# A decoder layer on one core: filling steps dealt by weight between attention steps, and one head group's last value product moved behind the branch products

## The chip, the cores and the metric

The kernel runs on one core of a Trainium2 chip. A core has a matrix engine (TensorE: PE in the profile, its weight loads as PEld), a vector engine (VectorE: DVE), an activation engine (ScalarE: ACT), a general engine (GpSimd: POOL) and a queue engine (SyncE: SP) that here only starts transfers. TensorE writes to PSUM, eight accumulators ("banks") of 128 x 512 float32 values; DVE and ACT read PSUM and write to the on-chip buffer SBUF. The metric is the device time of one execution in microseconds (us); lower is better.

## The reference, cut to what matters

One layer is computed for 512 tokens with 16 "meta" tokens ahead of them, model width 1024: a gated feed-forward (FFN) of inner width 2816, a token mixer, and a second FFN, each added to the residual. The change is inside the token mixer:

```python
qa, ka, va, fa, qb, kb, vb, ga, gb = jnp.split(h @ w_in, idx, axis=-1)   # q and k then RMS-normalised per head
# forgetting attention: 8 heads of 64, causal over the whole sequence
s = q @ k.T * scale + c[q] - c[k];      o_fox = softmax(mask(s)) @ v
# sliding attention: 8 query heads, 2 key/value heads, a band of 128 keys and the 16 meta tokens
s = q @ k.T * scale + bias;             o_swa = softmax_with_sink(mask(s)) @ v
y = sigmoid(ga) * (o_fox @ w_branch_fox) + sigmoid(gb) * (o_swa @ w_branch_swa)
return y @ w_out
```

All values are float32; a product is made as three TensorE passes on a high and a low part of each operand.

## The kernel before, in words

**Products.** Each operand x is kept as a high part (a rounded copy, made by ACT: `hi`, line 133 or 134) and a low part (x minus the high part, made by DVE: `lo`, lines 140 and 142). `prod` (lines 301, 302, 304) issues high x high, high x low and low x high into one PSUM bank. A weight piece lands by DMA in `raw`, is split by `hi` and `lo` into `wh` and `wl`, and is then used; `piece()` hands out the next piece and starts the loads and splits of later ones.

**Attention units.** The forgetting attention has eight units (four pairs of heads, and for each pair two pairs of query blocks), made by `fox_pair`. A unit is five steps: `scores` (products of queries with keys, line 1292; DVE adds the forgetting sums and finds the row minimum, line 1310; ACT takes exponentials, line 1209; DVE divides by the sums, line 1212), and then, for each of the two heads, `turn` (TensorE transposes the probabilities, lines 1337 and 1350; ACT and DVE split the result into `pH` and `pL`) and `values` (products with the values, lines 1359, 1364 and 1365; `both_halves`, lines 1105 and 1106, brings the two partition halves together into `oA`). The *first* `turn` of a unit is that of head 0, the *second* that of head 1. A unit of the later query blocks has seven transposes in its second `turn`, one of the earlier blocks three. The sliding attention has eight units of three steps (`swa_unit`): `scores` (DVE: line 1460), one `turn` for all four heads of a group (line 1473) and one `values` (lines 1488 and 1490).

**Stages and filling.** The units are dealt into four lists, `main[0]` to `main[3]`: four forgetting units, four more, four sliding units of group 0, four of group 1. The next unit's `scores` stands between the first `turn` of a unit and its first `values`. While an attention step waits for DVE and ACT, TensorE is to have other work: the lists in `fills`. Fills 0 to 2 are steps that project keys, queries, values and gates of later units (half a token block, or a quarter of a gate: 12 products of 256 columns or 6 of 512); fill 3 holds the 16 steps of the forgetting branch products (`foxes`: six products of 512 columns each, eight output blocks of two steps). `weave(main, fill)` writes the two lists into one: after main step i of n, the fills up to share i/n of their number.

**What sets the order.** The written order is a priority. The framework's planner lays each engine's instructions out ahead of the run on a modelled clock, so an instruction whose inputs it takes to be late can be passed by a later one of the same engine; it also assigns the buffers in the order in which they are given back. `after(i)` puts instructions behind i on their engine. On the chip each engine then keeps to its planned order.

**Behind the attention.** After the weaving come, in written order: sigmoids of three gate blocks `zA` on ACT (line 1653; the activation tables change here from exponential to sigmoid) and their products with the forgetting branch (DVE, line 1654); `stM.close()`, after which the stage's SBUF is used again by the pool `gates`, each tile as soon as the old tiles at its place are no longer used; differences of the mixer's input in `spare` (DVE, lines 1695 and 1696); the reload of the residual `xg` (two transfers on ACT's queue, line 1700); the last gate block's product, half before and half behind `split_o`, which splits the sliding result `oA` into `oW` and `oLs`; six sliding branch products, with copies back to `oA` (line 1722); scaling of `xg` (ACT, line 1728), sums of it (DVE, line 1732), their splits into S3, S2 and S1; and then the gate products (`seven`) that use S3 and the split sums `tc` of weights (lines 233 and 234).

**Places.** `spare` takes the place of transposed-probability inputs `t` and of the sliding values `v`; `xg` that of the two query buffers `qH`, one of which holds the low part of the forgetting result to the last of the branch products; the weight buffers `rawC` that of `pL`.

Of the kernel before, what the change touches and what calls it, by code (L numbers as in the profile page):

```python
# [55 lines left out]

def weave(main, fill):

    done, out = 0, []
    for i, f in enumerate(main):  # L60
        out.append(f)
        upto = (i + 1) * len(fill) // len(main)
        out += fill[done:upto]
        done = upto
    return out


def nothing():
# [8 lines left out]
def run(steps):  # L77
    for f in steps:
        f()
# [3 lines left out]
def kernel(  # L83
# [32 lines left out]
    def nm(s):  # L116
        nid[0] += 1
        return f"{s}_{nid[0]}"
# [489 lines left out]
    def after(*ins):  # L608

        st = ExitStack()  # L610
        for i in ins:
            st.enter_context(tc.issue_after(getattr(i, "ins", i)))
        return st
# [166 lines left out]
    def early(X, ff, dsts, second, sums, more, alone=0):  # L780


        u = [ff.plain(d, i == 0 and not alone) for i, d in enumerate(dsts)]
        main = u[0][:4] + u[1][:2]
        if alone:
            main[1:1] = [enter_rest]
        run(main[:alone] + second[:3] + main[alone:] + second[3:] if alone else weave(main, second))
        run(weave(u[0][4:] + [s for v in ([u[1][2:]] + u[2:]) for s in v], sums + more))
# [460 lines left out]
    def fox_pair(box, p, ip, before):  # L1249
# [115 lines left out]
                PE.matmul(pv[:, a:256], st, pL[:, c0 + a : c0 + 256], start=False, stop=j == nt - 1)  # L1365
            both_halves(oA[half[hh], 0, p, 2 * P * ip : 2 * P * (ip + 1)], half[hh], pv[:, :256])

        return [scores] + [lambda f=f, hh=hh: f(hh) for hh in range(2) for f in (turn, values)]

# [162 lines left out]
    for i in every:  # L1534
# [3 lines left out]
            out=zf[:n, i], in0=ps[:, 256:264], scalar=r1[:n, i : i + 1], in1=fb[:n], op0=ALU.mult, op1=ALU.add  # L1538
# [64 lines left out]
    def fox_out(m):  # L1603

        return zA[:, m] if m >= NG - 1 else oF["f"][m // 2][:, S * (m % 2) : S * (m % 2) + S]

    class Later:
# [10 lines left out]
    ]  # L1618
    parts = [
        [fox_pair(f0, p, ip, pre(p, ip)) for p in range(2) for ip in (1, 0)],  # L1620
        [fox_pair(f1, p, ip, pre(p, ip)) for p in range(2, 4) for ip in (1, 0)],
        [swa_unit(sw, q2, 0, i, swa_pre.get(i, nothing)) for i in range(NB)],
        [swa_unit(sw, q3, 1, i, nothing) for i in range(NB)],
# [11 lines left out]
    main = [[] for _ in parts]  # L1635
# [10 lines left out]
    run(main[0][:1] + fills[0][:2])  # L1646
    del main[0][:1], fills[0][:2]
    main[3].insert(0, fox_parts)
    for m, f in zip(main, fills):
        run(weave(m, f))  # L1650
    for m in range(NG - 1):
        with after(shared["exp"]):
            A.activation(zA[:, m], zA[:, m], AF.Sigmoid)
        V.tensor_tensor(out=zA[:, m], in0=zA[:, m], in1=fox_out(m), op=ALU.mult)
# [13 lines left out]
    part = lambda name: gp.tile([P, 2, 4, HF], F32R, tag=name, name=nm(name))  # L1668
# [352 lines left out]
```

## Time and profile before

| | |
|---|---|
| median of 3 runs | 1077.91 us (1076.78 to 1078.76) |
| profiled execution | 1075.97 us |
| its span, first to last instruction | 1074.2 us |
| TensorE matmul / weight loads, share of the span | 99% / 96% |
| DVE, ACT, POOL | 83%, 61%, 20% |
| granted TensorE clock | 0.999 |

The profiled execution lasts 1.77 us longer than its span. TensorE matmuls overlap: the start-to-start distance of two products of 256 columns is some 0.12 us while each is shown with 0.28 us, so a busy matmul row hides short waits, and a wait is read from the distance of starts. "[0.33 <-DVE pL L140]" behind an instruction says that its engine sat idle for 0.33 us until the DVE instruction of line 140 on `pL` was done. The attention with its filling runs from about 405 to 595 us, the last gate block and the sliding branch products from 595 to 618 us.

### The profile page before, as it was taken

Reading aid. Unit: us, or ns where it says so; the run is one execution under the profiler, and the core shown is the slowest. Engines: PE = TensorE matmul, PEld = TensorE weight load, DVE = VectorE, ACT = ScalarE, POOL = GpSimd, SP = SyncE. Lnnn points to the kernel's source line nnn. Section 1 sums busy time; section 2 is a strip of 40 time slices with the busy share of each in tenths; the row PEclk is TensorE's granted clock in tenths of the full one; section 3 lists DMA queues with packets and bytes.
Section 4 is the critical chain, followed back from the end, with each engine's and each line's share of the span. In section 5 each row is a group of like instructions: output and inputs, shape, how many; then the busy total and the mean of one; then the engine's idle time right before and its main releaser. Section 6 shows DMA issues by size and latency. Waiting matters only on the chain.

```text
span 1074.2 us, 22262 instructions
## 1 busy us (share of the span) xinstructions
PE 1062.6 (99%) x8515; PEld 1030.1 (96%) x8515; DVE 891.9 (83%) x1725; ACT 654.5 (61%) x1235; POOL 212.6 (20%) x281
## 2 busy tenths in 40 slices
PE   9999999999999999999999999999999999999998
PEld 8999999999999999999877799999999999999998
DVE  7988878888889678789897799778989788887895
ACT  7667456656666455556657776555665466745664
POOL 3011111121124442332200110001122211221120
PEclk9999999999999999999999999999999999999999
DMA  8787778688776314212211874556689777887763
GB/s 281 203 220 160 189 192 197 152 221 216 176 178 178 122 60 132 72 56 81 81 59 50 233 186 121 193 195 197 166 202 187 185 190 182 179 191 191 160 126 101
DMA packets 112570, 173.57 MB, mean 162 GB/s; under 512 B 10880, under 2 KB 59264, under 8 KB 112208
## 3 DMA queue, kind: packets, MB, share of 16 engines
q1 hardware_dynamic: 74464, 122.72, 36.0%
q0 software_dynamic: 29040, 37.83, 22.5%
q10 hardware_dynamic: 8960, 11.60, 3.4%
q8 instruction: 66, 1.08, 0.4%
q14 instruction: 40, 0.33, 0.1%
HBM read 167.89 MB, written 6.32 MB: 162 GB/s over the span
## 4 chain that ended last, share of the span: by engine, by line
PE 45%; DVE 4%; DMA 3%; ACT 3%; issue 1%; POOL 0%; ACTq 0%; DVEq 0%; POOLq 0%
PE ps L301 8%; PE ps L304 8%; PE ps L302 8%; PE pt L301 6%; PE pt L302 6%; PE pt L304 6%; DMA raw<-in_wout_dram 1%; DVE wl L140 1%; ACT wh L133 1%; DMA xg<-h1d 1%; ACT t L1209 1%; DVE pL L140 1%; ACT xg L1728 0%; PE ps L1473 0%; PE ps L1936 0%
## 5 line engine op out<-in xcount | busy, mean ns | idle before, releaser
L301 PE MATMUL ps<-x,wh 128*128 128x256 f32 (+2 forms) x768 | 219.9, 287 | 0.2
L302 PE MATMUL ps<-x,wh 128*128 128x256 f32 (+2 forms) x768 | 219.1, 285 | 0.5 <-DVE x L142 0.4
L304 PE MATMUL ps<-x,wl 128*128 128x256 f32 (+2 forms) x768 | 219.1, 286 | 0.0
L140 DVE TENSOR_TENSOR wl<-raw,wh 128x1024 fp32r<-128x1024 f32 (+3 forms) x125 | 150.0, 1201 | 39.7 <-ACT wh L133 38.4
L133 ACT CAST wh<-raw 128x1024 fp32r<-128x1024 f32 (+3 forms) x125 | 128.4, 1029 | 87.6 <-PE ps L302 50.9
L301 PEld LDWEIGHTS ps<-x,wh 128*128 128x128 f32 x768 | 144.9, 189 | 1.6 <-ACT hT L686 0.3
L302 PEld LDWEIGHTS ps<-x,wh 128*128 128x128 f32 x768 | 144.7, 188 | 1.4 <-DVE x L142 0.9
L304 PEld LDWEIGHTS ps<-x,wl 128*128 128x128 f32 x768 | 144.7, 188 | 0.8
L301 PE MATMUL pt<-x,wh 128*128 128x256 f32 (+2 forms) x424 | 125.4, 297 | 0.5 <-ACT wh L133 0.5
L304 PE MATMUL pt<-x,wl 128*128 128x256 f32 (+2 forms) x424 | 124.6, 295 | 0.0
L302 PE MATMUL pt<-x,wh 128*128 128x256 f32 (+2 forms) x392 | 112.7, 288 | 0.0
L133 ACT CAST wh<-tc 128x1024 fp32r<-128x1024 f32 (+1 forms) x70 | 71.8, 1026 | 65.4 <-DVE tc L234 56.1
L140 DVE TENSOR_TENSOR wl<-tc,wh 128x1024 fp32r<-128x1024 f32 (+1 forms) x70 | 83.5, 1193 | 32.4 <-ACT wh L133 32.2
L301 PE MATMUL ps<-acts,wh 128*128 128x264 f32 (+1 forms) x352 | 100.5, 286 | 0.1
L304 PE MATMUL ps<-acts,wl 128*128 128x264 f32 (+1 forms) x352 | 99.9, 284 | 0.0
L302 PE MATMUL ps<-acts,wh 128*128 128x264 f32 (+1 forms) x352 | 99.6, 283 | 0.0
L140 DVE TENSOR_TENSOR wl<-rawC,wh 128x1024 fp32r<-128x1024 f32 (+1 forms) x70 | 84.2, 1203 | 5.8 <-ACT wh L133 5.5
L133 ACT CAST wh<-rawC 128x1024 fp32r<-128x1024 f32 (+1 forms) x70 | 71.6, 1023 | 22.6 <-PE pt L302 16.7
L301 PEld LDWEIGHTS pt<-x,wh 128*128 128x128 f32 x424 | 80.0, 189 | 2.8 <-ACT wh L133 0.7
L304 PEld LDWEIGHTS pt<-x,wl 128*128 128x128 f32 x424 | 79.8, 188 | 2.1
L302 PEld LDWEIGHTS pt<-x,wh 128*128 128x128 f32 x392 | 73.8, 188 | 0.6
L301 PEld LDWEIGHTS ps<-acts,wh 128*128 128x128 f32 x352 | 66.6, 189 | 0.7 <-DVE h2T L918 0.3
(442 smaller groups left out, 3241.3 us busy)
## 6 DMA issues: line engine op xcount, KB each, us to landing
rawC<-in_w1i_dram SPq DMA_DIRECT2D x20, 512.0 KB, 4.3
raw<-in_w1i_dram SPq DMA_DIRECT2D x40, 256.0 KB, 4.6
raw<-in_w2i_dram SPq DMA_DIRECT2D x40, 256.0 KB, 3.5
rawC<-in_w2i_dram SPq DMA_DIRECT2D x20, 512.0 KB, 4.3
raw<-in_wm_dram SPq DMA_DIRECT2D x18, 512.0 KB, 4.2
raw<-in_wout_dram SPq DMA_DIRECT2D x16, 512.0 KB, 4.4
rawD<-in_w1i_dram SPq DMA_DIRECT2D x20, 256.0 KB, 3.9
raw<-in_w1i_dram POOLq DMA_DIRECT2D x20, 256.0 KB, 4.6
```

Source lines behind the costliest of these rows:

```text
L133: return A.copy(o, i)
L140: return V.tensor_tensor(out=o, in0=i, in1=h, op=ALU.subtract)
L301: PE.matmul(ps, sH, mH, start=first, stop=False, **more)
L302: PE.matmul(ps, sH, mL, start=False, stop=False, **more)
L304: shared["mm"] = PE.matmul(ps, sL, mH, start=False, stop=last, **more)
L1209: shared["exp"] = A.activation(t, t, AF.Exp, bias=nmx, scale=-1.0, accum_out=l[:, j : j + 1])
```

## The change: what it does

```diff
 def weave(main, fill):
 
-    done, out = 0, []
-    for i, f in enumerate(main):
+    done, out, part = 0, [], 0.0
+    share = [getattr(f, "share", 1.0) for f in main]
+    for f, s in zip(main, share):
         out.append(f)
-        upto = (i + 1) * len(fill) // len(main)
+        part += s
+        upto = len(fill) if f is main[-1] else int(part * len(fill) / sum(share) + 0.5)
         out += fill[done:upto]
         done = upto
     return out
+
+
+def shared_out(f, share):
+
+    def step():
+        f()
+
+    step.share = share
+    return step
...
-        return [scores] + [lambda f=f, hh=hh: f(hh) for hh in range(2) for f in (turn, values)]
+        shares = ((turn, 0, 1.0), (values, 0, 0.5), (turn, 1, 2.0), (values, 1, 0.5))
+        return [scores] + [shared_out(lambda f=f, hh=hh: f(hh), s) for f, hh, s in shares]
...
     main[3].insert(0, fox_parts)
+    last_values = main[3].pop()
     for m, f in zip(main, fills):
         run(weave(m, f))
+    last_values()
     for m in range(NG - 1):
```

A step now has a weight. A forgetting unit's second `turn` has 2, its two `values` 0.5 each, every other step 1, so a unit's sum stays 5; the fills are dealt by the weights gone by, rounded to the nearest instead of downward. Of the unit whose steps stand in the middle of `main[1]`, the written order goes from the first line to the second (F is a filling step, T and V the head's turn and values, S the next unit's scores):

```
before: T0 F S F V0 F T1 F V1 F
after:  T0 F S F V0 F T1 F F V1
```

Elsewhere the rounding moves single fills by one place; in `main[2]` the sliding steps keep the weight 1, and the first sliding turn has five fills behind its scores instead of four. The number of filling steps in each list, and every instruction, stay as they are.

Second, the last sliding unit's `values` leaves `main[3]` and is called after all steps of `foxes`. The end of that list goes, in written order, from the first line to the second (S15, T15 and V15 are the last sliding unit's steps, V14 the values of the one before, and 5b to 7b the branch products' steps):

```
before: S15 5b V14 6a T15 6b V15 7a 7b
after:  S15 6a 6b V14 7a T15 7b V15
```

## The prediction

> **What bounds the kernel now.** I read the page's head first, then the stages of the attention, then who TensorE waited for there.
>
> ```profile
> span 1074.2 us, 22262 instructions
> PE 1062.6 (99%) x8515; PEld 1030.1 (96%) x8515; DVE 891.9 (83%) x1725; ACT 654.5 (61%) x1235; POOL 212.6 (20%) x281
> ```
>
> TensorE is the bound over the whole run; only its waits can be won. The busy times of the two attention stretches:
>
> ```profile
> 405.00:530.00 125.00, 122.79 (x1022) 115.85 (x1021) 103.28 (x315) 73.81 (x188) 35.69 (x73) 1.00 0.28 85
> 530.00:595.40 65.40, 64.43 (x367) 50.63 (x366) 54.99 (x156) 45.15 (x113) 0.95 (x1) 1.00 0.18 58
> ```
>
> The columns are PE, PEld, DVE and ACT. Matmuls fill 122.79 of 125 us and 64.43 of 65.4 us, and DVE is busy for 83% and 84%: a second engine close behind. Next, PE's waits between 405 and 625 us, and then those of its weight loads:
>
> ```profile
> PE pt L1365 <- DVE pL L140: 1.0, 3, 0.5
> PE ps L1292 <- DVE qn L1073: 0.5, 1, 0.5
> PE pt L1488 <- ACT pH L133: 0.5, 1, 0.5
> PE pt L301 <- ACT wh L133: 0.5, 1, 0.5
> PE ps L301 <- ACT pt L529: 0.4, 1, 0.4
> PE ps L1473 <- DVE t L1212: 0.3, 1, 0.3
> ```
>
> ```profile
> PEld pt L1365 <- DVE pL L140: 2.1, 5, 0.7
> ```
>
> The longest wait is the one that the change is aimed at: value products (L1365) that wait for the low part `pL`. One of them, with its chain:
>
> ```profile
> 474.05 0.49 PE L1350 MATMUL ps<-ident,t 128*128 128x128 f32 x3
> ...
> 475.79 0.28 PE L1359 MATMUL pt<-pH,v 128*128 128x256 f32 x1
> ...
> 476.02 0.28 PE L301 MATMUL ps<-wh,x 128*128 128x256 f32 x1
> ...
> 477.10 0.38 PE L1365 MATMUL pt<-pL,v 128*128 128x256 f32 x1 [0.33 <-DVE pL L140]
> ...
> 474.88 0.48 ACT L133 CAST pH<-ps 128x384 fp32r<-128x384 f32 x1
> ...
> 475.65 0.60 DVE L1073 SCALAR_TENSOR_TENSOR qn<-hsq,r,hss 16x128 f32<-16x128 f32 x2
> 476.18 0.40 DVE L1106 TENSOR_TENSOR oA<-ps,hsq 64x256 f32<-64x256 f32 x1
> 476.51 0.54 DVE L140 TENSOR_TENSOR pL<-ps,pH 128x384 fp32r<-128x384 f32 x1
> ```
>
> The second transposition starts at 474.05, its values at 475.79, and the first product with `pL` at 477.10: 3.05 us after the transposition. `pH` was ready at 475.36, but DVE had a filling step's scaling (L1073) and an earlier head's sum (L1106) in its queue and came to `pL` 1.15 us later. At 476.02 the plan has let filling products (L301) pass the products with `pL`; it still took `pL` to be earlier than it was.
>
> **Part 1, the weights.** Behind a second transposition stand now one fill, afterwards two. A fill is the distance from the three transposes (0.25 us of starts) to 475.79: about 1.5 us, twelve products. Cover after the change: 1.74 + 1.5 = 3.24 us against the 3.05 needed; behind seven transposes it is half a microsecond more. So the five waits of the weight-load row (2.1 us) are covered, those behind three transposes with only 0.2 us in hand. I take -1.8: all of it, less a third of the 1.0 us or so that falls on units with three transposes. Bounds: -2.1 (all gone) and 0 (they come back elsewhere).
>
> What is taken away is half a fill behind each of the two value steps. The next unit's first transposition then follows its head's values closer, but keeps four fills behind its scores (one, a half, two and a half). Is it late next? The rows of the same unit:
>
> ```profile
> 474.90 0.83 DVE L1212 TENSOR_SCALAR t<-t,l 128x400 f32<-128x400 f32 x2
> ...
> 478.37 0.38 PE L1337 MATMUL pt<-ident,t 128*128 128x128 f32 x2
> ```
>
> Its probabilities are ready at 475.73 and are read at 478.37: 2.6 us in hand, more than the 0.5 us by which TensorE comes sooner. Cost nothing; without that cover it would be those 0.5 us per unit.
>
> The rounding also puts some fills half done ahead of a unit's scores, where they hold one more PSUM bank, and takes one away in other units. Scores of the later blocks take six banks. The row `ps L1292 <- DVE qn` (0.5) is such a wait, a bank that a filling step's scaling gives back. I take 0; bounds -0.5 (that wait gone) to +0.5 (one more like it). In `main[2]` the first sliding transposition gets a fifth fill behind its scores, so the 0.3 of L1473 goes: -0.3, bounds -0.3 and 0.
>
> **Part 2, the last values.** The rows from the last sliding transposition on:
>
> ```profile
> 587.51 0.60 PE L1473 MATMUL ps<-ident,t 128*128 128x128 f32 x4
> ...
> 587.91 1.28 ACT L1653 ACT_TABLE_LOAD   x1
> ...
> 589.20 0.63 ACT L1653 ACTIVATE zA<-zA 128x512 f32<-128x512 f32 x1
> ...
> 589.96 0.40 PE L304 MATMUL pt<-v,wl 128*128 128x512 f32 x1
> ...
> 590.25 0.58 ACT L133 CAST pH<-ps 128x512 fp32r<-128x512 f32 x1
> ...
> 590.89 0.50 PE L1488 MATMUL pt<-pH,v 128*128 128x512 f32 x1 [0.53 <-ACT pH L133]
> ...
> 591.23 0.40 PE L301 MATMUL ps<-v,wh 128*128 128x512 f32 x1
> ...
> 591.79 0.50 PE L1490 MATMUL pt<-pL,v 128*128 128x512 f32 x1 [0.17 <-DVE pL L140]
> ...
> 593.31 0.41 PE L1490 MATMUL pt<-pL,v 128*128 128x512 f32 x1
> ...
> 595.13 0.43 DVE L1106 TENSOR_TENSOR oA<-pt,hsq 64x256 f32<-64x256 f32 x1 [0.43 <-ACT hsq L1105]
> 595.17 0.40 PE L304 MATMUL ps<-v,wl 128*128 128x512 f32 x1
> ...
> 595.41 0.39 PE L301 MATMUL pt<-x,wh 128*128 128x512 f32 x1
> ...
> 595.66 0.69 DVE L1695 TENSOR_TENSOR spare<-x 128x512 f32<-128x512 f32 x1
> 595.69 0.82 ACTq L1700 DMA_DIRECT2D xg<-h1d  x2
> ```
>
> Products of 512 columns start 0.23 us apart. From 589.96 to 590.89 is 0.93, from 591.23 to 591.79 is 0.56: 0.70 + 0.33 = 1.03 us lost, because the table load (1.28) and a sigmoid stood ahead of `pH` on ACT. Afterwards the last transposition comes two fills of 1.4 us (six products of 0.23) later on TensorE, but the table load depends on the last exponentials, which come one fill later; so it has 1.4 us more to be out of the way. Behind the transposition stands 7b, and then the last gate block's products, which need nothing of it. I take -1.0; bounds -1.03 and 0.
>
> What is late next is `oA`. Now the last values' products are done at 593.7 and their sum at 595.56; with the waits gone TensorE comes to its end at 595.41 - 1.03 = 594.4 with the last values as last, and `oA` follows 1.85 us later, at 596.2. Everything that reads it must pass DVE:
>
> ```profile
> 600.34 1.89 DVE L140 TENSOR_TENSOR oLs<-oA,x 128x512 fp32r<-128x512 f32 x3
> ...
> 610.88 1.23 DVE L1732 TENSOR_TENSOR spare<-xg 128x1024 f32<-128x1024 f32 x1 [3.94 <-ACT xg L1728]
> ```
>
> The first low part `oLs` is done at 601.03 now, and TensorE, after 24 products of 0.232 us from 595.41, needs it at 601.2: nothing in hand. Afterwards it needs it at 600.2, and DVE, which also has `spare` to do (four of 0.6, a 1.2 and a weight split of 1.2), has it at about 600.4 to 601: I take +0.6, bounds 0 and +1.7 (`oA` 1.7 us later, if the waits stay and the last values end at 595.41).
>
> The third effect has the other sign. `xg` lies where the branch products' low operand was, and its transfer started at 595.69, as the last branch product (start 595.17) ended. That product now comes six products (1.4 us) and the waits (1.0) sooner, at about 593.2. The chain from there (ACT's scaling, the DVE row at 610.88 above, S3, the split sums) ends at these rows:
>
> ```profile
> 620.34 0.28 PE L304 MATMUL ps<-S,wl 128*128 128x256 f32 x1
> 621.00 0.38 PE L301 MATMUL ps<-S,wh 128*128 128x256 f32 x1 [0.38 <-ACT pt L529]
> ...
> 621.97 0.38 PE L301 MATMUL pt<-x,wh 128*128 128x256 f32 x1 [0.47 <-ACT wh L133]
> ```
>
> The waits of 0.4 and 0.5 there go if the chain comes 2 us sooner and TensorE only 0.4: -0.9. Bounds: -0.9 and +1.7 (the transfer behind the copies of `oA` on ACT's queue).
>
> **Sum.** -1.8 + 0 - 0.3 - 1.0 + 0.6 - 0.9 = -3.4 us. The profiled execution (1074.2 of span and 1.77 around it, 1075.97) becomes 1072.6. It is 1.94 us under the median of the runs, so the median becomes 1077.91 - 3.4 = **1074.5 us**.
>
> By the Trainium skill ("Perfetto Trace Analysis", Identifying the Most-Contended Engine) a matmul's busy share says little of the room left, and that of the weight loads is the measure. By it the two stretches hold 125 - 115.85 = 9.2 and 65.4 - 50.63 = 14.8 us of room, and a better order could win up to 24 us, several times my sum. This trace does not agree: PE's waits named above come to 3.2 us, and in the second stretch, where products have 512 columns, a load ends well ahead of its product without TensorE waiting for anything.
>
> **The rivals.** *The waits move.* Removed waits make TensorE come sooner to the next thing that DVE feeds; DVE is busy 83% of the stretch, and `pL` was late because of its queue, not for lack of ACT's part. For it: the 1.15 us at 475.36. Against it: the 2.6 us in hand at the transpositions. Terms 1 and 3 then give 0, the tail -1.3 to 0: 1076.6 to 1077.9.
>
> *The planner undoes it.* The written order is a priority only; at 476.02 the plan had already let filling products pass, where the change writes twelve more. If it places by its own clock either way, the waits stay as its errors: 1077.9, or 0.5 to either side.
>
> *The tail is later: slower.* The last transposition stands 2.8 us later, and from it to `oA` the old trace takes 587.51 to 595.56, 8.05 us. If that latency is ACT's and DVE's and does not shorten, `oA` is ready at 598.4, and `spare`, `oLs` and `rawC` all move by 2.8 us; TensorE has no work in hand at 601, and the waits at 620 are there already, so all of it is paid: 1077.9 + 2.8 = 1080.7, or 1078.9 with the first term won. It decides from the point at which `oA` ends 0.2 us (the reserve at 601) beyond TensorE's own gain. Against it: 1.9 of the 8.05 us are the table load and a sigmoid, which get 1.4 us of room, and four of `spare`'s operations can go ahead of `oA`.
>
> **How the numbers follow.** My forecast gets 0.56, waits that move 0.20, the planner 0.10, the later tail 0.14. About 0.2% (2.2 us) is what a measurement of this kernel can tell from no change. Faster by more than that: 0.53 of the forecast and 0.03 of the moved waits: 0.56. Slower: 0.11 of the tail's 0.14, and 0.02 of a moved wait that grows: 0.13. The rest, 0.31, is within. The forecast's own range is 1073.1 (-4.8: -2.1 - 0.5 - 0.3 - 1.03 + 0 - 0.9, every term at its best) to 1075.9 (-2.0: half a microsecond less of the first term, and the third effect nil). For 8 in 10 I take 1072.0 to 1079.7: below, the best sum and the 1.1 us by which a run of this kernel came out under its median; above, the later tail with the first term won (1078.9) and the 0.8 us by which one came out over it. So it holds the cases of no change, and leaves out the tail at its full price.
>
> **What would show it.** Right: no L1365 wait for `pL` behind a second transposition; no L1488 wait for `pH`; the last gate's products among or right behind the last values; the first `xg` transfer two to three microseconds ahead of the last `oA` sum; no wait at the first gate products. Wrong: waits of the same size at L1292, L1337 or L1350 (moved); the plan showing one fill behind second transpositions (undone); TensorE idle ahead of the first sliding product (L302 on `oLs`), or `xg` started behind `oA` (later tail).

## The result and the profile after

The change makes the kernel slower: 1083.93 us median (1079.42 to 1085.71, 9 runs) against 1076.36 us (1075.63 to 1078.76, 9 runs) of the kernel before in the same session, a ratio of 1.0061 with a 95% interval of 1.0050 to 1.0072: +7.6 us by the medians, +6.6 (5.4 to 7.8) by the ratio. The forecast of 1074.5 us (-3.4) was wrong in sign, and the time lies outside the range. The profiled execution is one of 1083.93 us. In the changed kernel, lines from `weave` on are 11 higher than before, those of the sliding units 12, those behind the attention 14.

Page head, and then the two attention stretches and three of the tail (columns PE, PEld, DVE, ACT, POOL, granted clock, DMA share, GB/s), all of the changed kernel:

```profile
span 1082.2 us, 22258 instructions
PE 1065.5 (98%) x8515; PEld 1032.2 (95%) x8515; DVE 893.4 (83%) x1725; ACT 655.7 (61%) x1235; POOL 213.5 (20%) x281
```

```profile
405.00:530.00 125.00, 123.45 (x1018) 116.15 (x1017) 103.09 (x315) 73.44 (x183) 35.56 (x72) 1.00 0.26 82
530.00:595.40 65.40, 63.51 (x371) 50.77 (x370) 54.32 (x153) 45.88 (x114) 1.53 (x2) 1.00 0.20 65
...
625.00:630.00 5.00, 2.13 (x14) 1.93 (x13) 4.78 (x5) 4.41 (x7) 0.86 (x1) 0.90 0.55 134
630.00:635.00 5.00, 5.00 (x36) 5.00 (x35) 4.16 (x7) 1.92 (x4) 0.12 (x1) 0.76 0.68 200
```

The number of matmuls is the same; in the first stretch PE shows more busy time (123.45 us for 122.79) with four products fewer. A busy matmul row is not a full TensorE, so the start times of TensorE's n-th matmul say more. They are read off both traces:

| matmul | where | before | after | later by |
|---|---|---|---|---|
| 3300 | first attention unit | 407.5 | 409.0 | 1.5 |
| 4200 | end of the forgetting units | 517.4 | 519.9 | 2.5 |
| 4500 | sliding units | 565.5 | 568.0 | 2.5 |
| 4700 | last gate block | 603.9 | 607.8 | 3.9 |
| 5000 | gate products | 647.5 | 655.7 | 8.2 |
| 8290 | second FFN | 1043.1 | 1051.1 | 8.0 |

So 1.5 us are lost ahead of the attention, 1.0 over the forgetting units, 1.4 from the middle of the sliding units to the last gate block and 4.3 in the tail behind it. Who TensorE waited for between 20 and 120 us (no such rows stand there before), and between 405 and 640 us (the four longest):

```profile
PE ps L312 <- ACT p L586: 0.7, 1, 0.7
PE ps L312 <- ACT pt L540: 0.2, 1, 0.2
```

```profile
PE ps L312 <- ACT pt L540: 2.9, 1, 2.9
PE pt L1485 <- DVE t L1223: 1.9, 2, 1.3
PE ps L315 <- DVE wl L151: 0.8, 1, 0.8
PE pt L313 <- issue: 0.6, 1, 0.6
```

The waits of value products for `pL` are gone. In their place stand sliding transpositions (L1485) that wait for probabilities, and in the tail waits for a weight split, for the first sliding product's `oLs` (the row "issue"; `oLs` is done at 604.8 and read at 604.97) and, the longest, for a copy on ACT. The tail's rows from the last transposition on:

```profile
593.70 0.60 PE L1485 MATMUL pt<-ident,t 128*128 128x128 f32 x4
...
596.39 0.40 PE L1500 MATMUL ps<-pH,v 128*128 128x512 f32 x1
...
598.10 0.50 PE L1502 MATMUL ps<-pL,v 128*128 128x512 f32 x1
598.67 0.40 PE L313 MATMUL pt<-x,wh 128*128 128x512 f32 x1
...
604.97 0.47 PE L313 MATMUL pt<-oLs,wh 128*128 128x512 f32 x1 [0.63 <-issue]
...
597.42 0.61 ACT L1629 COPY zA<-ps 128x512 f32<-128x512 f32 x1
...
600.44 0.84 ACTq L1714 DMA_DIRECT2D xg<-h1d  x2
...
599.94 0.43 DVE L1117 TENSOR_TENSOR oA<-ps,hsq 64x256 f32<-64x256 f32 x1 [0.43 <-ACT hsq L1116]
600.40 2.50 DVE L1709 TENSOR_TENSOR spare<-x 128x512 f32<-128x512 f32 x4
```

The last branch product's result is copied at 597.42, ahead of the last values' end. `xg`, which by the prediction only needs that, starts at 600.44: right behind the last `oA` sum (599.94 + 0.43), as does `spare` at 600.40. In the kernel before both ends fell together (last branch product 595.17 + 0.40, last sum 595.13 + 0.43), and the trace could not tell which one released `xg`. In the built program of both kernels the first `xg` transfer and the first `spare` operation wait for the last `oA` sum: the new pool's tiles start with the last use of the stage before, not each when its own place is free (the buffer that this sum reads lies at the place of neither). What the description of the kernel above says of that ("each tile as soon as the old tiles at its place are no longer used") is wrong.

### The profile page after: what moved, and what is told of

Its sections match the earlier page's. It is cut to its first block, busy times and chain, and to the rows that moved or that the text cites. A ratio compares the mean times of both kernels' runs of the same rounds, so it can differ in the third digit from the quotient of the medians.

```text
span 1082.2 us, 22258 instructions
## 1 busy us (share of the span) xinstructions
PE 1065.5 (98%) x8515; PEld 1032.2 (95%) x8515; DVE 893.4 (83%) x1725; ACT 655.7 (61%) x1235; POOL 213.5 (20%) x281
## 4 chain that ended last, share of the span: by engine, by line
PE 83%; DVE 7%; ACT 4%; DMA 3%; issue 1%; POOL 1%; SPq 0%; ACTq 0%; DVEq 0%
PE ps L312 14%; PE ps L313 14%; PE ps L315 14%; PE pt L312 12%; PE pt L313 12%; PE pt L315 11%; DVE wl L151 2%; ACT wh L144 1%; DMA xg<-h1d 1%; DMA raw<-in_wout_dram 1%; ACT t L1220 1%; DVE pL L151 1%; PE ps L1303 1%; PE pt L1303 1%; DMA xt<-in_x_dram 0%
```

## The experiments

Differences below are those of the medians in one session, with the ratio's interval behind them; where two runs of different sessions are compared, it is by their differences from the kernel before. The medians of the kernel before were 1076.01 to 1076.30 us in the four sessions.

**Which part is it?** Each part alone. From the changed kernel to the weights alone, and from the kernel before to the last values alone:

```diff
-    last_values = main[3].pop()
     for m, f in zip(main, fills):
         run(weave(m, f))
-    last_values()
```

> Only the weights: every list is dealt by them, the last sliding values stay inside the list of the branch products. Theory 'the tail': the large loss comes from the last values standing behind the branch products, because the next stage starts with their last sum; so here most of it is gone. Against 1076.4 us before: -2 for the waits behind second transpositions, +2 to +3 for waits ahead of sliding transpositions from the new rounding, +1.4 because the last sliding transposition stands one fill later: about 1078. Rival 'the weights': the new dealing alone makes the loss, and this is near the changed kernel's 1084.

Measured: 1078.70, +2.7 us (1.0014 to 1.0035).

```diff
+    last_values = main[3].pop()
     for m, f in zip(main, fills):
         run(weave(m, f))
+    last_values()
```

> Only the last values moved behind the branch products, dealt as before (all weights 1, rounded downward); the last sliding transposition stands two fills later than before. Theory 'the tail': the first residual transfer starts as the last sum of the last values ends, 3 to 4.5 us later than before's 595.7, TensorE waits 2 us or more at the first gate products, and the time is about 1081. Rival 'the weights': no change, 1076 to 1077.

Measured: 1080.83, +4.8 us (1.0029 to 1.0054). The last sliding transposition stands one filling step later than before in this kernel, not the two that the expectation names; in the whole change, with its rounding, it is two. Both parts lose, and their sum (7.5) is the whole's 7.6 within the noise.

**The weights: the shares or the rounding?** First the weights in the first two lists alone, the two others dealt as before and the last values in their place:

```diff
-        run(weave(m, f))
+        run((weave if j < 2 else weave_plain)(m, f))   # weave_plain: the old function
```

> The weights in the two lists of the forgetting attention alone; the two sliding lists dealt as before, the last values in place. If the waits for the low part behind second transpositions are won and nothing else moves: 1076.4 - 2 = 1074.4. If they come back as waits elsewhere: 1076.4.

Measured: 1077.49, +1.5 us (1.0009 to 1.0027): above both. The waits for `pL` were gone, and still it lost: 1.4 us at matmul 3300, where no list with weights has begun. That led to the callers of `weave`: it also deals the steps at the start of the feed-forward stages (`early`, lines 787 and 788 of the kernel before; in the first of them line 788 alone). There all shares are 1, but the count is now rounded to the nearest. So the rounding was tried without the weights, in all calls and in those two alone, and the weights without the rounding:

```diff
-        upto = (i + 1) * len(fill) // len(main)
+        upto = int((i + 1) * len(fill) / len(main) + 0.5)
```

> The old dealing with equal shares, only rounded to the nearest instead of down; no weights, the last values stay. Theory (the rounding costs): 1.2 us ahead of the attention, about 2 us where kv's last step comes ahead of the scores of the seventh unit, some 2 us at the sliding transpositions near 547 and 567 us, less up to 1 us for those second transpositions that get two fills by rounding alone: 1079 to 1081. Rival (the weights cost): within 0.5 us of before, 1076.

Measured: 1078.13, +2.0 us (1.0011 to 1.0028).

```diff
-        run(... if alone else weave(main, second))
-        run(weave(u[0][4:] + ..., sums + more))
+        run(... if alone else weave_near(main, second))   # weave_near: the function of the run before
+        run(weave_near(u[0][4:] + ..., sums + more))
```

> The kernel before with rounding to the nearest in the dealing of the first feed-forward stage and its like alone (the two calls in the function early); the attention is dealt as before. Theory: a wait of about 0.8 us for p near 45 us and a smaller one near 108 us come with it, 1.2 us in all: 1077.2. Rival (that wait in the runs with weights is noise, or comes from elsewhere): 1076.0.

Measured: 1077.44, +1.3 us, by the ratio +0.9 (0.9999 to 1.0017). The interval takes in no change. But the trace has the two waits shown above for 20 to 120 us (0.7 and 0.2 us), matmul 3300 starts 1.1 us later, and that distance stays to matmul 4700 (605.1 for 603.9).

```diff
-        upto = ... int(part * len(fill) / sum(share) + 0.5)
+        upto = ... int(part * len(fill) / sum(share) + 0.001)   # weights alone, rounded down
```

> The weights in all four lists as in the change, but the number of fills that are due is rounded down, as before, and not to the nearest; the last values stay in their list. The dealing ahead of the attention (where all shares are 1) and that of the sliding stages are then those of before. Theory (the rounding is what costs; the weights themselves win): no wait for pL behind a second transposition, kv's last step behind the scores of the seventh unit again, no wait of 0.8 us near 45 us; the 2.1 us of those waits are won: 1074.0, some 2.0 us under before. Rival (the waits move whatever the rounding): within 0.7 us of the kernel before, like the run with weights in the first two lists less the loss ahead of the attention, 1076.0 to 1076.5.

Measured: 1075.60, -0.5 us (0.9986 to 1.0005). With e1 (+2.7) this puts the rounding at 3.2 us. The weights themselves win less than was thought, and by the times that win is not clear of noise; in the trace matmul 4500 starts 0.7 us sooner and 3300 0.4 later, 1.1 us won between them.

Where the rounding costs inside the attention was tried by exchanging two written steps in this kernel: kv's last step (the end of the keys' and values' projection) with the seventh unit's scores, and the first quarter of the second gate block (the expectation calls it the first half) with the third sliding unit's scores.

```diff
+        if j == 1:   # the other kernel: j == 2, gates[4], parts[2][2][0]
+            k = steps.index(kv[-1])
+            assert steps[k - 1] is parts[1][2][0]
+            steps[k - 1 : k + 1] = [steps[k], steps[k - 1]]
...
```

> The weights rounded down, with two written steps exchanged: the last step of kv (its norms, ten transpositions and conversions) stands ahead of the scores of the seventh fox unit, where the rounding to the nearest had put it, instead of behind them. Theory: the conversions then stand ahead of those scores on ScalarE's and VectorE's queues, the two halves of the scores start one after the other and not in pairs, and TensorE loses about 1.9 us between 492 and 501 us: 1077.5. Rival (that stretch costs the same in either order, the loss of the run with weights in the first two lists came from another fill): 1075.6.

Measured: 1078.07, +1.9 us (1.0008 to 1.0026) and 2.4 over the weights rounded down. The rows of that unit's score products, grouped by line, and the stretch around them, with kv's step behind (first) and ahead (second):

```profile
L1303 PE MATMUL pt<-kH,qH x6: 273/284/445, 493.2 to 494.5; 64*128 64x400 f32 x2, 64*128 64x272 f32 x2, 64*128 64x256 f32 x2
L1303 PE MATMUL ps<-kH,qH x6: 278/360/446, 493.2 to 495.9; 64*128 64x400 f32 x2, 64*128 64x272 f32 x2, 64*128 64x256 f32 x2
...
491.00:501.00 10.00, 10.00 (x86) 9.36 (x85) 9.20 (x33) 6.58 (x18) 2.68 (x7) 1.00 0.24 71
```

```profile
L1303 PE MATMUL pt<-kH,qH x6: 276/312/447, 494.5 to 496.4; 64*128 64x400 f32 x2, 64*128 64x272 f32 x2, 64*128 64x256 f32 x2
L1303 PE MATMUL ps<-kH,qH x6: 272/360/446, 497.4 to 500.0; 64*128 64x400 f32 x2, 64*128 64x272 f32 x2, 64*128 64x256 f32 x2
...
491.00:501.00 10.00, 9.90 (x66) 8.19 (x66) 7.38 (x24) 5.17 (x14) 1.89 (x3) 1.00 0.21 66
```

The score products use 64 of the 128 rows, each head of a pair the other half. Behind the usual steps the two heads' first products start together (493.2 and 493.2) and run side by side; with kv's conversions ahead of them the second head comes only when the first is done (497.4 behind 496.4). TensorE stays 99% busy by the profile (9.90 of 10 us) and starts 66 products instead of 86. Matmul 4200 starts 2.3 us later than with the weights rounded down (519.4, 517.1).

> The weights rounded down, with two written steps exchanged: the first half of the second gate block (g1.0, which brings a weight split of 1.0 us on ScalarE and 1.2 us on VectorE with it) stands ahead of the scores of the third sliding unit instead of behind them. Theory (the split stands ahead of the unit's softmax on VectorE's queue): a wait of 1.3 us for the probabilities at the sliding transposition near 546 us, and 1077.0 in all. Rival (the wait came from the unit having had other fills): no such wait, 1075.6.

Measured: 1076.40, +0.2 us (0.9996 to 1.0014), 0.7 over the weights rounded down. By the times that is not clear of noise; in the trace matmul 4500 starts 1.1 us later (565.9, 564.8). So the loss is there, but not as one wait of 1.3 us. In the changed kernel that wait stands behind this order on DVE; the first two rows are those of the kernel before:

```profile
540.43 0.43 DVE L1460 CUSTOM_DVE_ANT_0 t<-pt,cb 128x273 f32<-128x273 f32 x1
...
541.88 1.22 DVE L140 TENSOR_TENSOR wl<-raw,wh 128x1024 fp32r<-128x1024 f32 x1
```

```profile
542.73 1.22 DVE L151 TENSOR_TENSOR wl<-raw,wh 128x1024 fp32r<-128x1024 f32 x1
543.86 0.44 DVE L1472 CUSTOM_DVE_ANT_0 t<-ps,cb 128x273 f32<-128x273 f32 x1
...
546.72 1.17 DVE L1223 TENSOR_SCALAR t<-t,l 128x273 f32<-128x273 f32 x4
...
547.23 0.51 PE L1485 MATMUL pt<-ident,t 128*128 128x128 f32 x2 [1.30 <-DVE t L1223]
```

A weight split that the moved fill brings along stands ahead of the softmax's first operation; before, the split came behind it. That a split ahead of the scores delays a sliding transposition is shown in this trace; why the one exchanged step spreads the loss over several places stays open.

**The last values: which end of the tail?** The last values behind all branch products again, but with the old dealing, so that the last transposition is not moved:

```diff
+        if j == 3:
+            steps.remove(m[-1])
+            steps.append(m[-1])
...
```

> The order of before, but the last sliding values are taken out and called behind the last two branch steps; the last sliding transposition stays where it was. Theory 'the tail starts with the last sum': TensorE comes to the last values about 1.7 us later than before, so the residual's transfer starts about 1.7 us later and the time is 1078 to 1079. If the lateness of the transposition is what counts, this is within 0.5 us of before.

Measured: 1080.33, +4.3 us (1.0029 to 1.0055), nearly as much as with the transposition moved (4.8): the place of the values is what costs. Its trace holds the chain. ACT's order ahead of the gate products and the transfers' row (median from issue to landing) of the kernel before, and then the same of this one, with the last sum, TensorE's products that stand behind a wait, and the stretch behind them:

```profile
619.62 1.05 ACT L133 CAST wh<-tc 128x1024 fp32r<-128x1024 f32 x1 [1.15 <-DVE tc L234]
620.58 0.37 ACT L529 COPY pt<-ps 128x256 f32<-128x256 f32 x1
620.88 1.04 ACT L133 CAST wh<-rawC 128x1024 fp32r<-128x1024 f32 x1
...
xg<-h1d ACTq DMA_DIRECT2D x2, 1024.0 KB, 10.2
```

```profile
596.63 0.43 DVE L1106 TENSOR_TENSOR oA<-ps,hsq 64x256 f32<-64x256 f32 x1 [0.43 <-ACT hsq L1105]
...
597.13 0.84 ACTq L1704 DMA_DIRECT2D xg<-h1d  x2
...
601.66 0.47 PE L302 MATMUL pt<-oLs,wh 128*128 128x512 f32 x1 [1.27 <-DMA rawC<-in_wg_dram]
...
619.63 0.39 PE L304 MATMUL ps<-x,wl 128*128 128x256 f32 x1 [1.01 <-DVE wl L140]
...
625.35 0.45 PE L301 MATMUL ps<-S,wh 128*128 128x256 f32 x1 [2.86 <-ACT pt L529]
...
622.55 1.04 ACT L133 CAST wh<-tc 128x1024 fp32r<-128x1024 f32 x1 [3.02 <-DVE tc L234]
623.50 0.58 ACT L1726 COPY oA<-pt 128x512 f32<-128x512 f32 x1
623.98 1.05 ACT L133 CAST wh<-rawC 128x1024 fp32r<-128x1024 f32 x1
624.92 0.37 ACT L529 COPY pt<-ps 128x256 f32<-128x256 f32 x1
...
xg<-h1d ACTq DMA_DIRECT2D x2, 1024.0 KB, 11.0
...
625.00:630.00 5.00, 4.65 (x26) 4.65 (x27) 4.27 (x4) 3.14 (x7) 0.00 (x0) 0.66 0.79 156
```

The last sum ends 1.5 us later than before (597.06 for 595.56; 0.3 of it is a later start of the whole attention), and `xg` with it (597.13 for 595.69). TensorE then waits 1.4 us for `oLs` (the row names a transfer of `rawC`; the first `oLs` is done at 601.4, and the product starts at 601.66). The transfer takes 0.8 us longer; beside it, the fourth of the large transfers of the gate stage's weights starts 1.4 us behind it now (the second row here), where 4.6 us lay between them before (the first):

```profile
600.28 0.43 SPq L206 DMA_DIRECT2D rawD<-in_wg_dram  x1
```

```profile
598.48 0.44 SPq L206 DMA_DIRECT2D rawD<-in_wg_dram  x1
```

The sums of `xg` are 2.9 us late, so is `tc`, and `wh` of `tc` holds up ACT, where the copy L529 that TensorE needs now stands behind a second cast as well: 624.92 for 620.58. TensorE's next products start 3.0 us late behind it, where it was 0.5. Ahead of that stands a wait of 1.0 us for a weight split that comes late on DVE with the sums, and behind it the granted clock is at 0.66 over 5 us, 1.7 us lost. Together that is the trace's tail: 1.4 + 1.0 + 3.0 + 1.7 us, less the values' 1.0 and the 0.9 that the gate products waited before, is 5.2, where the distance from matmul 4600 to 8290 grew by 5.1.

Half the dose, the last values behind one of the two half steps:

```diff
+        if j == 3:
+            k = steps.index(m[-1])
+            steps[k : k + 2] = [steps[k + 1], steps[k]]
...
```

> The kernel before, with the last values behind one of the two last half steps of the branch products, not behind none (before) or both (the run with V15 behind 7a and 7b, 4.3 us slower). If what counts is the moment at which oA is complete, counted from where the last branch product ends, most of a fill (1.4 us, less the 1.0 us of waits that the values lose by coming later) is paid once at the first sliding product and again in the gate stage's first sums: 1077.0 to 1078.5. If only the very last place is bad (the planner's order on ScalarE's queue behind it): 1076 or below, as the values' waits of 1.0 us go.

Measured: 1076.27, +0.1 us (0.9991 to 1.0008). Its rows; this execution runs 1.6 us behind that of before from its first stages on (its granted clock is 0.83 between 10 and 20 us, 1.7 us lost), and the last transposition starts at 589.10 for 587.51:

```profile
589.10 0.60 PE L1473 MATMUL ps<-ident,t 128*128 128x128 f32 x4
...
596.70 0.43 DVE L1106 TENSOR_TENSOR oA<-ps,hsq 64x256 f32<-64x256 f32 x1 [0.43 <-ACT hsq L1105]
...
597.21 0.84 ACTq L1705 DMA_DIRECT2D xg<-h1d  x2
```

From the transposition's start to the sum's 7.60 us pass, before 7.62: the values' waits (1.0 us) go, one half step (six products, 1.4 us) takes their place, the sum is complete at the same moment, and nothing is lost. The second half step, in e4, is what makes it late.

And the table load that made the values wait, moved behind their `pH`:

```diff
-                hi(pH, ps)
+                shared["last_pH"] = hi(pH, ps)
...
-        with after(shared["exp"]):
+        with after(shared["exp"], shared["last_pH"]):
```

> The kernel before; only the sigmoids behind the attention, and with them the table load of 1.28 us, are issued behind the hi part pH of the last transposition. If the 1.03 us of waits of the last values (L1488, L1490) are that table load's, as the prediction had it, they go and the sum oA, the transfer xg and everything behind them come 1.0 us sooner: 1075.0. If the products wait for something else as well, or DVE's products with the sigmoids come behind the last sums: 1076.0 or a little above.

Measured: 1076.57, +0.4 us (0.9995 to 1.0013). No L1488 or L1490 wait is left, and nothing is won: the sigmoids and their products on DVE (L1654) come later in turn, and stand ahead of the last `oA` sum, which starts 597.84 - 590.10 = 7.74 us behind the transposition instead of 7.62.

**Does it add up, and is it the clock?** The whole change, rounded down:

> The whole change, weights and last values, but with the number of due fills rounded down. Theory (the parts add): 0.5 us below before for the weights, 4.3 to 4.8 above for the last values, 1080.0; so the rounding is 3.9 us of the change's loss. Rival (in the changed kernel the rounding and the last values cost the same waits twice): 1083.

Measured: 1081.19, +4.9 us (1.0032 to 1.0056). Against the change's +7.6 the rounding is 2.7 us (by the ratios 1.8); the parts add.

In the changed kernel's trace the granted clock falls right behind the 3-us wait (0.90 and 0.76 in the rows above: (0.10 + 0.24) x 5 = 1.7 us lost, so 1.7 of the 4.3 us that this execution loses in the tail). TensorE was given twelve products in that wait:

```diff
             use("P7", c[:, :th])
+            if twice:                      # the first gate unit
+                d = psum(True)
+                product(d, "S3", w, 1)     # again, into the bank that ACT overwrites
```

> The changed kernel with twelve products more: the first gate unit's S3 product is done a second time, into a bank that ScalarE overwrites afterwards, so that TensorE has 1.4 us of work in its wait of 3.0 us near 626 us; the output is the same. Theory (after that wait TensorE runs at half the granted clock for 3.4 us, which is part of the loss): the wait splits into a shorter one, the granted clock stays at 1.0 there, and the median falls by about 1.7 us, to 1082.2, with most runs at a mean clock of 0.999 or above. Rival (the clock falls for another reason, or the runs differ by something else): the median stays at 1083.9 or rises by up to 1.4 us.

Measured: 1084.45, +8.2 us (1.0058 to 1.0084). The clock stayed up in the profiled execution:

```profile
625.00:630.00 5.00, 3.56 (x30) 3.36 (x30) 4.78 (x6) 4.25 (x7) 0.86 (x1) 1.00 0.54 135
630.00:635.00 5.00, 5.00 (x45) 5.00 (x44) 4.86 (x8) 2.88 (x7) 0.68 (x1) 1.00 0.70 220
```

The time did not fall with it: near the end (400 matmuls before the last) TensorE was 0.9 us ahead of the changed kernel, and a wait of 1.9 us for the copy of an output block (0.5 there) gave that back. The executions' mean clocks do not settle it either: the changed kernel took 1079.42 and 1080.11 us at 0.999 and above and 1082.27 to 1085.71 below, while this one took 1083.55 us and more in four of its five at 0.999 and above. How much of the change's loss is the clock's stays open. It is not the main part of what the last values lose: e2's four executions with a mean clock of 1.0 have a median of 1080.4 and e4's three one of 1080.2, both more than 4 us above the kernel before.

**What the runs point to.** The second values exchanged with the fill behind them, everything else left in its place; and this with the last values behind one half step:

```diff
+        for k in range(len(steps) - 2, -1, -1):
+            if getattr(steps[k], "second", False) and any(steps[k + 1] is g for g in f):
+                steps[k : k + 2] = [steps[k + 1], steps[k]]
...
```

> The kernel before, with one edit: each second values step of a fox unit changes places with the fill behind it. So two fills stand behind the second transpositions, as in the change, but every other step keeps its place, and nothing is rounded. Theory: the waits for pL behind second transpositions go (1.0 us of TensorE's own waits in the profile of before), nothing else moves: 1075.0. Rival (the waits move to the next thing that VectorE feeds): 1076.0.

Measured: 1075.41, -0.8 us (0.9982 to 1.0000). In the trace no wait for `pL` is left between 405 and 530 us, and 1.0 us is won between matmuls 3300 (408.1) and 4500 (565.1).

> What the runs point to as best: the second values steps exchanged with the fill behind them (0.8 us under before), and the last values behind one half step of the branch products (0.1 us over before, with their waits of 1.0 us gone). If both waits stay away and nothing follows: 1074.8. If the second edit gives nothing: 1075.4.

Measured: 1075.30, -1.0 us (0.9982 to 1.0000). Both lie below the kernel before, at the edge of what can be told; the second edit adds nothing that can be measured.

## Why the prediction was wrong

**The first term (-1.8) had the right mechanism and the wrong size.** The waits for `pL` went, as "what would show it" had it. But the term was taken from the weight loads' row (2.1 us, five waits), where the matmuls' own row said 1.0 us, three waits. A load waits ahead of its product, so part of its wait lies beside products that still run. The traces gave 1.0 (one fill exchanged) and 1.1 us (weights rounded down). The 0.3 of L1473 was put down to the first sliding transposition and its fifth fill; in the trace before, the first starts at 526.81 without a wait, and the 0.3 stand at the second (535.00).

**"I take 0; bounds -0.5 to +0.5" for the rounding is the step that failed in Part 1.** It cost about 3 us (3.2 without the last values, 1.8 to 2.7 with them). Three things were missed. `weave` has two calls outside the attention, so the count of moved fills was not complete (about 1 us). A fill was priced by a PSUM bank; but it carries its split, its norms and its conversions, and what it overtakes on ACT and DVE is the scores' softmax (0.7 to 1.1 us at one gate step). And TensorE's work was taken to be the same in any order, while the scores of two heads run side by side or one after the other (2.3 us).

**Part 2 took the stall for the price.** The values' waits (-1.0) can be taken away, and e10 did so without gain: what sets the tail is when `oA` is complete, and that depends on ACT's and DVE's order. `oA`'s term (+0.6, bounds 0 and +1.7) was counted once, at the first sliding product, where 0.6 us (the changed kernel) and 1.4 us (e4) were waited.

**"The third effect has the other sign" is the step that failed in Part 2: its premise was wrong.** `xg` does not start as the last branch product ends; it waits for the last use of the whole stage, the `oA` sum. Instead of -0.9 it is a second payment for the same lateness: the wait at the gate products went from 0.5 to 3.0 us, with the weight split's 0.8 to 1.0 ahead of it.

**The rival "the tail is later" was the right one**, with a chance of 0.14, and its signs came: `xg` behind `oA`, TensorE idle ahead of the first sliding product. Its condition holds too (nothing is lost while the sum is not later, e14). Its price of 2.8 us was too small and its place not quite right. It let the moved transposition carry the loss, where e4 loses nearly the same without moving it, and passed the delay on as it was, where the longer transfer, the copy behind two casts and in some executions the clock make 4.3 to 4.9 us of it. "The waits move" came true too, at the sliding transpositions, through the rounding and not through TensorE's haste. The planner did not undo the change: the waits for `pL` are gone.

## What to carry to other kernels

Where a rule that deals out work is changed, list all its callers and every place that moves, and price a moved step by what it issues on the other engines and by what it overtakes there, not by TensorE's own work. Before an edit near the end of a stage is credited with the stall that it removes, find what the next stage waits for: when a whole pool is released by the last use of the old one, the last small operation of the stage starts everything, and a stall ahead of it may be free. Try the cheapest version of an idea first: here the second values exchanged with the fill behind them did at least as well as the weights (0.8 us, at the edge of what can be told, for 0.5) and moved nothing else.

## What had not been expected of the hardware

Products on 64 rows of two heads run side by side when both are ready: 86 products in 10 us against 66 when they come one after the other, with TensorE 100% and 99% busy by the profile. The Trainium skill ("TensorE: Matmul & The Clock Gate", Part 3: Packing small matmuls) states that products in different row groups of the array overlap; the pairs' equal starts (493.2 us) agree.

Behind the same wait (2.9 us without a product) the granted clock fell in the changed kernel, in e4 and in e18, each time by 1.7 us' worth: at 0.50, as the changed kernel's trace has it from 630 to 632 us, that is 3.4 us. It did not fall in e2's profiled execution:

```profile
623.40 1.04 ACT L133 CAST wh<-tc 128x1024 fp32r<-128x1024 f32 x1 [3.03 <-DVE tc L234]
...
625.00:630.00 5.00, 3.79 (x32) 3.79 (x33) 4.77 (x5) 3.92 (x7) 0.69 (x1) 1.00 0.62 130
630.00:635.00 5.00, 5.00 (x45) 5.00 (x44) 4.48 (x10) 2.92 (x6) 1.58 (x2) 1.00 0.60 157
```

It also fell without such a wait: from about 12 us on it is 0.50 for 3.4 us in e14's trace and for 6.8 us (twice 3.4) in those of e8, e10 and e18, with no wait of TensorE above 0.6 us since the transpositions of the input began near 8 us, and it is 1.00 there in all the others. So an early fall of the clock is part of what sets two executions apart, whatever the edit.

The Trainium skill ("TensorE: Matmul & The Clock Gate", What's actually happening) gives a window of 3413 ns that runs freely and half rate behind an idle one; the length of 3.4 us and the 0.50 agree. A whole such window does not fit into a wait of 2.9 us, so the page's words alone do not explain the fall there; that the window's place against the wait decides, which would let one trace show it and another not, is tested by no run here.
